# Moving the side stream's transfers and the merges' loads from SyncE's queue to GpSimd's

## The chip, the cores and the metric

The kernel runs on one core of one Trainium2 chip. The metric is the time of one execution on the device in microseconds (us); a kernel is timed in several runs, and one execution more is taken by the hardware profiler. The engines are TensorE (PE), VectorE (DVE), ScalarE (ACT), GpSimd (POOL) and SyncE (SP). Each has its own instruction stream and works in order. A DMA is issued by an instruction in the stream of SP, ACT or POOL, which waits there until what the transfer needs (its data, its free buffer) is there; everything behind it in that stream waits too.

## The reference

One encoder layer and a final norm on two independent sequences (`x_prompt`, `x_sample`) of 1024 tokens by 1024 features, float32:

```python
h = rmsnorm(x, norm1_g)
u_h, q, k, v, g_h, g_a = split(h @ w_in)
filt = hyena_filters(...)             # small MLP with sines, times a decay
y_h = hyena_mixer(u_h, ..., filt)     # short conv, then two rounds of: FFT convolution, times a gate
y_a = window_attention(rope(q), rope(k), v, sink)   # 8 heads, 2 kv heads, blocks of 128
merged = sigmoid(g_h) * (y_h @ w_up_hyena) + sigmoid(g_a) * (y_a @ w_up_attn)
x = x + merged @ w_out
h = rmsnorm(x, norm2_g)
x = x + (silu(h @ w_ff_gate) * (h @ w_ff_up)) @ w_ff_down
return rmsnorm(x, final_g)
```

## The kernel before

Every large product is done in three float32r matmuls (`row`, lines 716 to 718): weight and input are split into a high part (cast on ACT, line 465) and a low rest (subtraction on DVE, line 466).

The program has a main stream and a side stream, both Python generators, which `mix` weaves into one program order with a rate for each stage. The order of each engine's instructions is this program order.

- The main stream is the projections of sample 0, then of sample 1 (`proj_u`, `proj_qkv`, `proj_gates`), the merges (`merge_up`, `merge_out`) for four half sequences, and the two feed-forward blocks. Weights come in tiles of 512 KB through three buffers (`weights`, line 704, on SP).
- The side stream runs beside the projections and the first merges: `filters` (the filter MLP, then the spectra of the filters, stored to memory as `kd`), `hyena(0)`, `attention(0)`, `hyena(1)`, an early part of the merge, and `attention(1)`.

What the change touches:

- Filters: `wo` (line 405) and `dcy` (line 418) share five buffers (`DB = 5`); DVE multiplies the product of `wo` with `dcy` (line 419). `hb` is a bias row. `keep` copies each spectrum group to `ks` (two buffers, lines 427 and 428 on ACT) and stores it to `kd` (line 434).
- `mats` (line 482) loads the 8 matrices of one discrete Fourier transform, `dft_f` or `dft_i`; three times `dft_f`, twice `dft_i`.
- Convolutions: for each of 8 groups, `back` loads the stored spectrum `K` (line 572, two buffers, `KB = 2`), and DVE multiplies with it (line 575). `x2` (line 645) is the second gate, and `yh` (line 649) the stored result; the load of the input `z` and of the first gate `x1` stay on SP.
- Attention: `qb` (line 1071, two buffers) is a block of queries, `ya` (line 1164) the stored result; the loads of all keys and values (`kv`, lines 1065 and 1066) stay on SP.
- Merges: `pair_of` (line 1681) loads two rows of gates (`gin`) or of residuals (`xres`) into the tag `t4`, which has three buffers (`TB = 3`) and also holds squares. ACT applies tanh to the gate tile (line 1187), DVE multiplies it with the product in PSUM (line 1197), adds the two branches (line 1200), and the sum is split again (lines 465 and 466). The rows of `yh` and `ya` come through `y_row` (line 1173, on SP), the finished residual goes out as `xs` (line 1215, on SP). `early_merge` (lines 1049 and 1051) loads the first rows and the first gate ahead.

Issued by POOL already are the loads of the feed-forward input (`sides_in`, line 1297, tile `r`), in the last third of the program. All other DMAs are on SP, but for three on ACT at the start.

The framework that builds the program places the waits: an instruction waits on semaphores that other engines and the DMAs count up. `dynamic_dma_scratch_size=1024` is the room for POOL's transfer descriptors.

Of the kernel before, what the change touches and what calls it, by code (L numbers as in the profile page):

```python
# [21 lines left out]
P = 128  # L22
# [13 lines left out]
CH = 256  # L36
# [14 lines left out]
HALVES = (slice(0, 512), slice(512, 1024))  # L51
# [205 lines left out]
class Kern:  # L257
# [138 lines left out]
    def filter_spectra(self, cpool, hs):  # L396
        nc, a = self.nc, self.a
        mf = self.mats(cpool, "dft_f")
        self.full.clear()
        for o in range(2):  # L400
            ws = []
            for d in range(2):
                wo = cpool.tile([P, DH], F32, tag="dcy", name="wo", bufs=DB)
                for r in range(2):
                    nc.sync.dma_start(wo[64 * r:64 * r + 64], a["filt_w_out"][0].rearrange("k (d o c) -> k d o c", d=2, o=2)[:, d, o])
                ws.append(self.split(cpool, wo, [P, DH], f"ws{d}", bufs=1))
            yield 1.0
            for h in range(2):
                kt = cpool.tile([P, 16, CH], F32, tag="kt", name="kt")
                for r in range(2):  # L410
                    for j in range(0, 8, 2):
                        ps = self.psm()
                        for i in range(2):
                            for k in range(2):
                                nc.tensor.matmul(ps[:, CH * i:CH * i + CH], hs[r][:, P * (j + i):P * (j + i) + P], ws[r][k][:, CH * h:CH * h + CH], start=(i == 0 and k == 0), stop=(k == 1), skip_group_check=i > 0)
                        s = slice(8 * r + j, 8 * r + j + 2)
                        dcy = cpool.tile([P, 2, CH], F32, tag="dcy", name="dcy", bufs=DB)
                        nc.sync.dma_start(dcy, a["decay"][h, :, s])
                        nc.vector.tensor_tensor(kt[:, s], ps.rearrange("p (i c) -> p i c", i=2), dcy, ALU.mult)
                        yield KY  # L420
                hb = cpool.tile([1, CH], F32, tag="hb", name="hb", bufs=1)
                nc.sync.dma_start(hb, a["hyena_bias"][:, o, CH * h:CH * h + CH])
                nc.vector.tensor_tensor(kt[0:1, 0], kt[0:1, 0], hb, ALU.add)

                def keep(g, X, dst=self.kd[o][h]):
                    ks = cpool.tile([P, 4, CH], F32, tag="ks", name="ks", bufs=2)
                    nc.scalar.copy(ks[:, 0:3:2], X)
                    nc.scalar.activation(ks[:, 1], X[:, 1], AF.Copy, scale=-1.0)
                    if g == 0:
                        nc.scalar.copy(ks[:, 3], X[:, 0])  # L430
                        nc.vector.tensor_copy(ks[0:1, 3], X[0:1, 1])
                        nc.vector.memset(ks[0:1, 1:3], 0.0)
                    n = 4 if g == 0 else 3
                    nc.sync.dma_start(dst[:, g, :n], ks[:, :n])
                    yield 0.0

                sx = cpool.tile([P, 8, CH], F32, tag="sx", name="sx")
                for part, op in ((0, ALU.add), (1, ALU.subtract)):
                    nc.vector.tensor_tensor(sx, kt[:, 0:8], kt[:, 8:16], op)
                    yield 2.4  # L440
                    for p in self.spectrum(cpool, sx, part, mf, keep):
                        yield p if isinstance(p, float) else 1.1
# [34 lines left out]
    def mats(self, pool, name):  # L477

        m = {}
        for g in (0, 4, 2, 6, 1, 7, 3, 5):  # L480
            m[g] = pool.tile([P, 4 if g == 0 else 3, P], F32, tag=f"{name}{g}", name=f"{name}{g}", bufs=1)
            self.nc.sync.dma_start(m[g], self.a[name + "0"][0] if g == 0 else self.a[name][g - 1])
        return m

    def spectrum(self, pool, x, part, mf, then):
# [77 lines left out]
    def conv(self, pool, z, o, h, fm, mf, mi, late=None):  # L563
        nc = self.nc
        B = {}

        def tmp(tag, n):
            return pool.tile([P, n, CH], F32, tag=tag, name=tag, bufs=1)

        def back(g, X):  # L570
            K = pool.tile([P, 3, CH], F32, tag="K", name="K", bufs=KB)
            nc.sync.dma_start(K, self.kd[o][h][:, g, 0:3])
            t1 = pool.tile([P, 2, CH], F32, tag="t1", name="t1", bufs=YB)
            t2 = pool.tile([P, 2, CH], F32, tag="t2", name="t2", bufs=1)
            nc.vector.tensor_tensor(t2, X[:, ::-1], K[:, 1:3], ALU.mult)
            yield 0.4
            if g == 0:
                Kd = pool.tile([P, CH], F32, tag="Kd", name="Kd", bufs=1)
                nc.sync.dma_start(Kd, self.kd[o][h][:, 0, 3])
                nc.vector.tensor_tensor(t1[:, 0], X[:, 0], K[:, 0], ALU.mult)  # L580
                nc.vector.tensor_tensor(t1[:, 1], X[:, 1], Kd, ALU.mult)
            else:
                nc.vector.tensor_tensor(t1, X, bc(K[:, 0], 2, 1), ALU.mult)
            yield 0.4
            nc.vector.tensor_tensor(t1, t1, t2, ALU.add)
            ys = self.both(pool, t1, g, "Ys")
            yield LAG_Y
            if not fm:
                r = yield from self.dft("sb", mi[g], t1, ys, g)
                B[g] = pool.tile([P, 2, CH], F32, tag="B", name="B", bufs=4)  # L590
                nc.scalar.copy(B[g], r)
            else:
                r = yield from self.dft_across("sb", mi[g], t1, ys, g)
                B[g] = pool.tile([P, 2, CH], F32, tag="B", name="B", bufs=4)
                nc.scalar.copy(B[g].rearrange("p c (t n) -> p t c n", t=2), r)

        y = pool.tile([P, 8, CH], F32, tag="z", name="y", bufs=2)
        for part in range(2):
            groups = []
            for p in self.spectrum(pool, z, part, mf, back):  # L600
                if isinstance(p, float):
                    yield p
                    continue
                groups.append(p)
                if len(groups) < 4:
                    yield 3.3 if len(groups) > 1 else 1.0
            if part and late:
                late()
            for p in groups[:2]:
                yield p  # L610
            st = inv_even(nc, B, y, tmp) if part == 0 else inv_odd(nc, B, y, tmp)
            for c in st:
                if c is None:
                    break
                yield c
            for p in groups[2:]:
                yield p
            for c in st:
                yield c or 0.5
        return y  # L620
# [5 lines left out]
    def convolutions(self, pool, s):  # L626
        nc = self.nc
# [11 lines left out]
        for h in range(2):  # L639
# [2 lines left out]
            y = yield from self.conv(pool, zs[h], 0, h, False, mf, mi)  # L642
            nc.vector.tensor_tensor(y, y, x1, ALU.mult)
            x2 = pool.tile([P, 2, 8, P], F32, tag="gx", name="gx", bufs=1)
            nc.sync.dma_start(x2, self.x2f[s][2 * h:2 * h + 2].rearrange("t p (n m) -> p t n m", n=8))
            yield 1.5
            yf = yield from self.conv(pool, y, 1, h, True, mf, mi, None if h else lambda: load(1))
            nc.vector.tensor_tensor(x2, x2, yf.rearrange("p n (t m) -> p t n m", t=2), ALU.mult)
            nc.sync.dma_start(self.yh[s][2 * h:2 * h + 2].rearrange("t p (n m) -> p t n m", n=8), x2)
            yield 1.5  # L650


# [389 lines left out]
    def early_merge(self, pool, into, rows):  # L1042

        nc = self.nc
# [1 line left out]
        yy = self.yy.__enter__()  # L1046
        raw = [pool.tile([P, 2, 512], F32, tag=t, name="yraw", bufs=1) for t in ("rf", "ar")]
        for i, t in enumerate(raw):
            nc.sync.dma_start(t, self.yh[0][2 * i:2 * i + 2, :, HALVES[0]].rearrange("j p n -> p j n"))
        g = yy.tile([P, 2, 512], F32, name="gin")  # L1050
        nc.sync.dma_start(g, self.gt[0][0:2, :, HALVES[0]].rearrange("j p n -> p j n"))
        into.append(g)
        yield 0.4
        for t in range(4):
# [7 lines left out]
    def attend(self, pool, s):  # L1062
        nc = self.nc
# [3 lines left out]
        qs = {}  # L1067

        def load(b):
            qs[b] = pool.tile([P, 8, HD], F32, tag="qb", name="qb", bufs=2)  # L1070
            nc.sync.dma_start(qs[b], self.qkv[s][:, b, 0:512].rearrange("p (h e) -> p h e", h=8))

        load(0)
        vv = pool.tile([P, NB, NKV, 2, HD], F32R, name="vv")
# [8 lines left out]
        for b0 in range(0, NB, 4):  # L1083
# [3 lines left out]
            q = slice(P * b0, P * b0 + 512)  # L1087
# [18 lines left out]
    def heads(self, pool, s, b, g, qb, kh, kl, vv):  # L1106

        nc = self.nc
# [52 lines left out]
        for r in range(2):  # L1161
            f = lambda t: t.rearrange("p (a r q) -> p a r q", a=2, r=2)[:, :, r]
            nc.vector.tensor_tensor(oo[64 * r:64 * r + 64], f(po[0:64]), f(ol), ALU.add)
        nc.sync.dma_start(self.ya[s][2 * g:2 * g + 2, :, P * b:P * b + P].rearrange("t p q -> p t q"), oo)


    def y_row(self, yp, tmp, u, i, t):
# [432 lines left out]
    def main(self, outs):  # L1600
# [69 lines left out]
        with tc.tile_pool(name="pb", bufs=TB, reuse_waits="tile") as tmp:  # L1670
# [3 lines left out]
            with tc.tile_pool(name="ya", bufs=1, reuse_waits="tile") as yp, tc.tile_pool(name="ma", bufs=1, reuse_waits="tile") as pool:  # L1674
                def pair_of(c, u, jp):
# [2 lines left out]

                    def load():
                        t = tmp.tile([P, 2, 512], F32, tag="t4", name="xres" if c == "o" else "gin")  # L1680
                        nc.sync.dma_start(t, src[:, :, tok].rearrange("j p n -> p j n"))
                        return t

                    return load
# [144 lines left out]
```

## Time and profile before

| | |
|---|---|
| time, median of 3 runs | 2856.88 us (2856.84 to 2857.31) |
| profiled execution: time | 2856.86 us |
| its span, first to last instruction | 2855.1 us |
| mean granted TensorE clock | 0.997 |
| PE busy | 2822.5 us, 99% |
| DVE busy | 2109.1 us, 74% |
| ACT busy | 1226.2 us, 43% |
| POOL busy | 74.9 us, 3% |
| DMA of SP's queue (q1) | 435.04 MB |
| DMA of POOL's queue (q0) | 73.41 MB |

Busy time is the share of the span in which an engine worked on an instruction; issuing a DMA and waiting are not counted for SP. Matmuls overlap in the pipeline, so a PE that is 99% busy may still start fewer of them than it could, and the number of matmuls started in a stretch says more. A row of waits names the engine and the line that waited, what it waited for, the total, how often, and the longest wait. In a timeline row stand start, duration, engine, line and operation, and in brackets the idle time before it and what ended it. For DMAs, the landing is the time from the issue until the data has arrived.

### The profile page before, as it was taken

The page shows a single profiled execution, that of the slowest core. Times are in us where ns is not written, and L with a number is a line of the kernel's source. Part 1 is how long each engine was busy: PE and PEld are TensorE (multiplying, and loading weights), DVE is VectorE, ACT ScalarE, POOL GpSimd, SP SyncE. Part 2 cuts the span into 40 slices and gives each one's busy share as a digit, 9 for nine tenths or more (in the row PEclk, how much of TensorE's full clock was granted, in tenths as well). Part 3 has the DMA queues.
Part 4 walks back from the last instruction along what each step waited for, and adds up shares of the span by engine and source line. Part 5 has one row for each costly group of instructions (what it writes and reads, how often), then busy time and mean ns, then how long its engine had stood idle before and what let it go on. Part 6 is the DMA issues. An engine that isn't in the chain of part 4 may idle for free.

```text
span 2855.1 us, 36264 instructions
## 1 busy us (share of the span) xinstructions
PE 2822.5 (99%) x13522; PEld 2337.8 (82%) x13522; DVE 2109.1 (74%) x3395; ACT 1226.2 (43%) x1996; POOL 74.9 (3%) x146
## 2 busy tenths in 40 slices
PE   9999999999999999999999999999999999999998
PEld 7789888888898888777787888888888888888887
DVE  7987887877768887978686767775656766676566
ACT  6444222348743334887444444443122444443122
POOL 0000000000000000000000000001112000001100
PEclk9999999999999999999999999999999999999999
DMA  5566564442154435545674436558466434448631
GB/s 164 176 223 243 188 214 156 163 137 82 66 181 128 158 124 186 170 138 176 217 232 163 155 118 223 219 222 307 179 243 258 162 118 152 154 159 323 267 147 67
DMA packets 204029, 510.90 MB, mean 179 GB/s; under 512 B 18663, under 2 KB 70027, under 8 KB 203853
## 3 DMA queue, kind: packets, MB, share of 16 engines
q1 hardware_dynamic: 183261, 435.04, 44.3%
q0 software_dynamic: 20160, 73.41, 6.5%
q8 instruction: 107, 1.75, 0.3%
q14 instruction: 69, 0.57, 0.1%
q10 hardware_dynamic: 432, 0.14, 0.0%
HBM read 350.69 MB, written 157.83 MB: 178 GB/s over the span
## 4 chain that ended last, share of the span: by engine, by line
PE 84%; DVE 6%; DMA 4%; ACT 4%; issue 1%; SPq 0%; DVEq 0%; ACTq 0%
PE mm L716 8%; PE mm L717 8%; PE mm L718 8%; PE mm L1344 4%; PE mm L1346 4%; PE mm L1345 4%; PE sc L529 2%; PE mm L1546 1%; PE mm L1547 1%; PE mm L1545 1%; PE mm L993 1%; PE mm L994 1%; PE sb L1346 1%; PE sb L1345 1%; PE sb L1344 1%; PE mm L992 1%
## 5 line engine op out<-in xcount | busy, mean ns | idle before, releaser
L465 ACT CAST whi<-raw 128x1024 fp32r<-128x1024 f32 (+3 forms) x274 | 265.5, 970 | 524.1 <-PE mm L717 167.2
L466 DVE TENSOR_TENSOR wlo<-raw,whi 128x1024 fp32r<-128x1024 f32 (+3 forms) x274 | 306.4, 1119 | 152.7 <-ACT whi L465 152.1
L716 PE MATMUL mm<-hh,whi 128*128 128x512 f32 x872 | 360.0, 413 | 1.7 <-ACT hh L848 1.6
L718 PE MATMUL mm<-hh,wlo 128*128 128x512 f32 x872 | 349.8, 401 | 0.0
L717 PE MATMUL mm<-hl,whi 128*128 128x512 f32 x872 | 349.5, 401 | 0.0
L465 ACT CAST whi<-s 128x1024 fp32r<-128x1024 f32 x104 | 109.2, 1050 | 251.1 <-PE mm L1345 59.7
L1346 PE MATMUL mm<-r,wlo 128*128 128x512 f32 x518 | 201.6, 389 | 0.0
L1345 PE MATMUL mm<-r,whi 128*128 128x512 f32 x518 | 201.6, 389 | 0.0
L1344 PE MATMUL mm<-r,whi 128*128 128x512 f32 x518 | 201.5, 390 | 0.0
L716 PEld LDWEIGHTS mm<-hh,whi 128*128 128x128 f32 x872 | 164.3, 189 | 33.1 <-ACT hh L848 2.4
L718 PEld LDWEIGHTS mm<-hh,wlo 128*128 128x128 f32 x872 | 164.2, 188 | 33.0 <-issue 0.2
L717 PEld LDWEIGHTS mm<-hl,whi 128*128 128x128 f32 x872 | 164.6, 189 | 29.8 <-issue 0.5
L466 DVE TENSOR_TENSOR wlo<-s,whi 128x1024 fp32r<-128x1024 f32 x104 | 127.0, 1221 | 14.7 <-ACT whi L465 14.1
L1297 POOL DMA_DIRECT2D r<-comb x112 | 59.4, 530 | 2581.2 <-PE mm L1346 1965.2
L1344 PEld LDWEIGHTS mm<-r,whi 128*128 128x128 f32 x518 | 97.2, 188 | 20.7 <-ACT c L1411 0.4
L1345 PEld LDWEIGHTS mm<-r,whi 128*128 128x128 f32 x518 | 97.3, 188 | 20.1
L1346 PEld LDWEIGHTS mm<-r,wlo 128*128 128x128 f32 x518 | 97.2, 188 | 20.1
L994 PE MATMUL mm<-whi,hl 128*128 128x256 f32 x384 | 112.0, 292 | 0.0
L993 PE MATMUL mm<-wlo,hh 128*128 128x256 f32 x384 | 110.5, 288 | 0.0
L992 PE MATMUL mm<-whi,hh 128*128 128x256 f32 x384 | 109.5, 286 | 0.0
L716 PE MATMUL mm<-yh,whi 128*128 128x512 f32 x256 | 101.8, 400 | 4.2 <-DVE gin L1197 2.8
L717 PE MATMUL mm<-yl,whi 128*128 128x512 f32 x256 | 101.6, 397 | 3.5 <-DVE yl L466 3.5
(583 smaller groups left out, 7136.6 us busy)
## 6 DMA issues: line engine op xcount, KB each, us to landing
r<-comb POOLq DMA_DIRECT2D x112, 512.0 KB, 9.4
comb<-stage SPq DMA_DIRECT2D x48, 1024.0 KB, 4.9
K<-kd SPq DMA_DIRECT2D x64, 384.0 KB, 3.2
raw<-in_w_fg SPq DMA_DIRECT2D x44, 512.0 KB, 4.5
raw<-in_w_fu SPq DMA_DIRECT2D x44, 512.0 KB, 3.6
raw<-in_w_g SPq DMA_DIRECT2D x32, 512.0 KB, 3.6
gt<-ge SPq DMA_DIRECT2D x32, 512.0 KB, 3.0
raw<-in_w_up SPq DMA_DIRECT2D x32, 512.0 KB, 4.0
```

What stands on the lines that cost most here:

```text
L465: self.nc.scalar.copy(hi, src)
L466: self.nc.vector.tensor_tensor(lo, src, hi.bitcast(F32), ALU.subtract)
L716: mm(ps, hi[:, k], xh[:, s], start=first, stop=False)
L717: mm(ps, hi[:, k], xl[:, s], start=False, stop=False)
L718: mm(ps, lo[:, k], xh[:, s], start=False, stop=last)
L992: nc.tensor.matmul(ps[:, q], xh[:, t], wh, start=(i == 0), stop=False)
L993: nc.tensor.matmul(ps[:, q], xh[:, t], wl, start=False, stop=False)
L994: nc.tensor.matmul(ps[:, q], xl[:, t], wh, start=False, stop=(i == 7))
L1297: self.nc.gpsimd.dma_start(t.bitcast(F32), src[q][PLACE[name]])
L1344: mm(ps, hi[:, k], xh, start=(first and k == 0), stop=False, skip_group_check=not first)
L1345: mm(ps, hi[:, k], xl, start=False, stop=False, skip_group_check=not first)
L1346: mm(ps, lo[:, k], xh, start=False, stop=(k == n - 1), skip_group_check=not first)
```

## The change

Fourteen calls of `nc.sync.dma_start` become `nc.gpsimd.dma_start`; nothing else differs. With them the listed transfers are issued by POOL's stream, in the same order among themselves. Sizes, buffers and the program order stay.

```diff
@@ filter_spectra
-  nc.sync.dma_start(wo[64 * r:64 * r + 64], a["filt_w_out"][0]...)
+  nc.gpsimd.dma_start(wo[64 * r:64 * r + 64], a["filt_w_out"][0]...)
-  nc.sync.dma_start(dcy, a["decay"][h, :, s])
+  nc.gpsimd.dma_start(dcy, a["decay"][h, :, s])
-  nc.sync.dma_start(hb, a["hyena_bias"][:, o, CH * h:CH * h + CH])
+  nc.gpsimd.dma_start(hb, a["hyena_bias"][:, o, CH * h:CH * h + CH])
-  nc.sync.dma_start(dst[:, g, :n], ks[:, :n])
+  nc.gpsimd.dma_start(dst[:, g, :n], ks[:, :n])
@@ mats
-  self.nc.sync.dma_start(m[g], self.a[name + "0"][0] if g == 0 else self.a[name][g - 1])
+  self.nc.gpsimd.dma_start(m[g], self.a[name + "0"][0] if g == 0 else self.a[name][g - 1])
@@ conv, back
-  nc.sync.dma_start(K, self.kd[o][h][:, g, 0:3])
+  nc.gpsimd.dma_start(K, self.kd[o][h][:, g, 0:3])
-  nc.sync.dma_start(Kd, self.kd[o][h][:, 0, 3])
+  nc.gpsimd.dma_start(Kd, self.kd[o][h][:, 0, 3])
@@ convolutions
-  nc.sync.dma_start(x2, self.x2f[s][2 * h:2 * h + 2]...)
+  nc.gpsimd.dma_start(x2, self.x2f[s][2 * h:2 * h + 2]...)
-  nc.sync.dma_start(self.yh[s][2 * h:2 * h + 2]..., x2)
+  nc.gpsimd.dma_start(self.yh[s][2 * h:2 * h + 2]..., x2)
@@ early_merge
-  nc.sync.dma_start(t, self.yh[0][2 * i:2 * i + 2, :, HALVES[0]]...)
+  nc.gpsimd.dma_start(t, self.yh[0][2 * i:2 * i + 2, :, HALVES[0]]...)
-  nc.sync.dma_start(g, self.gt[0][0:2, :, HALVES[0]]...)
+  nc.gpsimd.dma_start(g, self.gt[0][0:2, :, HALVES[0]]...)
@@ attend
-  nc.sync.dma_start(qs[b], self.qkv[s][:, b, 0:512]...)
+  nc.gpsimd.dma_start(qs[b], self.qkv[s][:, b, 0:512]...)
@@ heads
-  nc.sync.dma_start(self.ya[s][2 * g:2 * g + 2, :, P * b:P * b + P]..., oo)
+  nc.gpsimd.dma_start(self.ya[s][2 * g:2 * g + 2, :, P * b:P * b + P]..., oo)
@@ main, pair_of
-  nc.sync.dma_start(t, src[:, :, tok].rearrange("j p n -> p j n"))
+  nc.gpsimd.dma_start(t, src[:, :, tok].rearrange("j p n -> p j n"))
```

More of the change, by code (lines that the diff above doesn't have):

```diff
@@ L404, in filter_spectra @@
                 for r in range(2):
-                    nc.sync.dma_start(wo[64 * r:64 * r + 64], a["filt_w_out"][0].rearrange("k (d o c) -> k d o c", d=2, o=2)[:, d, o])
+                    nc.gpsimd.dma_start(wo[64 * r:64 * r + 64], a["filt_w_out"][0].rearrange("k (d o c) -> k d o c", d=2, o=2)[:, d, o])
                 ws.append(self.split(cpool, wo, [P, DH], f"ws{d}", bufs=1))
@@ L644, in convolutions @@
             x2 = pool.tile([P, 2, 8, P], F32, tag="gx", name="gx", bufs=1)
-            nc.sync.dma_start(x2, self.x2f[s][2 * h:2 * h + 2].rearrange("t p (n m) -> p t n m", n=8))
+            nc.gpsimd.dma_start(x2, self.x2f[s][2 * h:2 * h + 2].rearrange("t p (n m) -> p t n m", n=8))
             yield 1.5
@@ L648, in convolutions @@
             nc.vector.tensor_tensor(x2, x2, yf.rearrange("p n (t m) -> p t n m", t=2), ALU.mult)
-            nc.sync.dma_start(self.yh[s][2 * h:2 * h + 2].rearrange("t p (n m) -> p t n m", n=8), x2)
+            nc.gpsimd.dma_start(self.yh[s][2 * h:2 * h + 2].rearrange("t p (n m) -> p t n m", n=8), x2)
             yield 1.5
@@ L1048, in early_merge @@
         for i, t in enumerate(raw):
-            nc.sync.dma_start(t, self.yh[0][2 * i:2 * i + 2, :, HALVES[0]].rearrange("j p n -> p j n"))
+            nc.gpsimd.dma_start(t, self.yh[0][2 * i:2 * i + 2, :, HALVES[0]].rearrange("j p n -> p j n"))
         g = yy.tile([P, 2, 512], F32, name="gin")
-        nc.sync.dma_start(g, self.gt[0][0:2, :, HALVES[0]].rearrange("j p n -> p j n"))
+        nc.gpsimd.dma_start(g, self.gt[0][0:2, :, HALVES[0]].rearrange("j p n -> p j n"))
         into.append(g)
@@ L1070, in load @@
             qs[b] = pool.tile([P, 8, HD], F32, tag="qb", name="qb", bufs=2)
-            nc.sync.dma_start(qs[b], self.qkv[s][:, b, 0:512].rearrange("p (h e) -> p h e", h=8))
+            nc.gpsimd.dma_start(qs[b], self.qkv[s][:, b, 0:512].rearrange("p (h e) -> p h e", h=8))
         load(0)
@@ L1163, in heads @@
             nc.vector.tensor_tensor(oo[64 * r:64 * r + 64], f(po[0:64]), f(ol), ALU.add)
-        nc.sync.dma_start(self.ya[s][2 * g:2 * g + 2, :, P * b:P * b + P].rearrange("t p q -> p t q"), oo)
+        nc.gpsimd.dma_start(self.ya[s][2 * g:2 * g + 2, :, P * b:P * b + P].rearrange("t p q -> p t q"), oo)
     def y_row(self, yp, tmp, u, i, t):
```

## The prediction

> **What bounds the kernel now.** I read the page first, then the busy time by stretch, then who makes TensorE (PE) wait, and last the chain.
>
> ```profile
> span 2855.1 us, 36264 instructions
> ...
> PE 2822.5 (99%) x13522; PEld 2337.8 (82%) x13522; DVE 2109.1 (74%) x3395; ACT 1226.2 (43%) x1996; POOL 74.9 (3%) x146
> 1400.00:1500.00 100.00, 95.64 (x423) 77.91 (x421) 85.17 (x120) 53.72 (x72) 0.00 (x0) 1.00 0.70 228
> 2000.00:2100.00 100.00, 98.31 (x434) 81.12 (x433) 57.00 (x67) 16.90 (x17) 19.05 (x36) 1.00 0.63 242
> 2300.00:2400.00 100.00, 100.00 (x443) 82.81 (x442) 69.59 (x90) 43.41 (x58) 0.00 (x0) 1.00 0.42 147
> ```
>
> PE is busy for 2822.5 of 2855.1 us, so it idles 32.6 us in all, start and end included. That is the whole purse: moving transfers can't win more. In an undisturbed stretch PE starts 443 matmuls in 100 us; between 1400 and 1500, in the merges, it starts 423 and idles 4.4 us. The change reaches PE only through waits like these:
>
> ```profile
> PE mm L717 <- DVE yl L466: 3.5, 3, 1.6
> PE mm L716 <- DVE gin L1197: 2.8, 1, 2.8
> ...
> PE mm L716 <- ACT yh L465: 1.4, 1, 1.4
> ...
> PE tr L776 <- DVE ns L753: 0.4, 1, 0.4
> ```
>
> Columns: total, times, longest (us). All four rows are in the merges. ScalarE (ACT) works in order: its tanh on a gate tile (gin, L1187) waits for that tile's load, and the cast of a y row (yh) behind it, or the VectorE (DVE) work that needs the gate, comes late. The next fence shows it: ACT's total wait for gate loads and that for weights of the projections, and the first and the last of five gate loads (4 to 6 us each, at 1186, 1315, 1396, 1417 and 1492 us) among the longest pieces of the chain that ended last (start, length).
>
> ```profile
> ACT gin L1187 <- DMA gin<-gt: 23.0, 11, 4.4
> ...
> ACT whi L465 <- DMA raw<-in_w_u: 0.2, 1, 0.2
> 1186.55 3.80 DMA gin<-gt
> ...
> 1492.84 5.78 DMA gin<-gt
> ```
>
> Weights do not appear this way: 0.2 us is all that ACT or DVE wait for a weight of the projections or merges. So what SyncE's (SP's) queue holds up in front of the weights costs nothing visible today, and taking it away wins nothing there.
>
> **The change part by part.** No work goes. By the table of DMA issues, 294 transfers leave SP's queue for POOL's: 64 K, 8 Kd, 32 kd stores, 32 dcy, 4 hb, 8 wo, 40 dft matrices, 4 x2 loads, 4 yh stores, 3 of the early merge, 31 gin, 16 xres, 16 qb and 32 ya stores. The order among the moved ones stays, so each is behind fewer others than before. POOL's own loads of r start at 1964.6 us, some 400 us after the last moved one, and are not delayed. What a moved transfer pays is a later issue and another landing:
>
> ```profile
> L1681 SPq DMA_DIRECT2D gin<-gt x8: 360/374/462, 1385.8 to 1427.7; - x8
> DMA to landing us min/median/max: 4.4/5.4/5.6
> L1297 POOL DMA_DIRECT2D r<-comb x112: 527/527/670, 1964.6 to 2718.8; - x112
> r<-bs POOLq DMA_DIRECT2D x1, 512.0 KB, 3.5
> r<-comb POOLq DMA_DIRECT2D x1, 512.0 KB, 5.0
> r<-comb POOLq DMA_DIRECT2D x1, 512.0 KB, 7.8
> 2086.54 0.39 PE L1547 MATMUL mm<-r,wlo 128*128 128x512 f32 x1
> 2087.34 0.53 POOL L1297 DMA_DIRECT2D r<-comb  x1 [2.87 <-PE mm L1547]
> 1416.58 0.69 DVE L466 TENSOR_TENSOR ml<-gin,mh 128x512 fp32r<-128x512 f32 x1
> 1417.29 0.38 SPq L1681 DMA_DIRECT2D gin<-gt  x1
> ```
>
> The first two rows are eight gate loads on SP between 1380 and 1440 (issue in ns, landing in us); the third is POOL's issue; then the landing of the first load of a POOL burst, with nothing of its queue before it, at 2141, 2021 and 1964 us. Issue time: 294 x 0.527 = 155 us of POOL in some 1450 us, hidden, as POOL has no other work there; if that cover were gone, it would be those 0.53 us for each. From release to issue SP takes 0.02 us (1416.58 + 0.69 = 1417.27, then 1417.29), POOL 0.41 (2086.54 + 0.39 = 2086.93, then 2087.34). From issue to landing, 512 KB take 4.4 to 5.6 (middle 5.4) on SP in this dense stretch and 3.5 to 7.8 (middle 5.0) on POOL. So the extra latency d of a gate load lies between 0.41 + 3.5 - 5.42 = -1.5 and 0.41 + 7.8 - 4.42 = +3.8 us; the middles give 0.0. The POOL row of 5.0 is from a stretch with 242 GB/s, nearest to the merges' 228. But a gate load has two rows of 2 KB for each partition where r has one of 4 KB, a form that no row of POOL shows; one more 0.53 us of issue for it would make d 0.5. I round up, because POOL's burst of 1964 is long: d = 0.6.
>
> By the Trainium skill, DMA: Bandwidth & Descriptors, section "Latency and other measured facts", the first byte comes some 1 us after a POOL issue and some 0.6 us after an SP one. With POOL's later issue that is an estimated d of 0.8, and the sum below would be 1.0 us higher; the middles here, 5.0 on POOL against 5.4 on SP, don't show that difference under load.
>
> Merges: five waits of PE follow a late gate load and have no slack left, since PE already waits: yl twice (the third yl wait, at 1177, follows ACT's own work), yh, gin and ns. Each grows by d: 5 x 0.6 = 3.0 us. The load at 1186.55 is on the chain without such a wait after it; half counts, 0.3. The xres loads are issued a product pair ahead and nobody waits for one: nothing, or 0.6 each if that cover goes.
>
> ```profile
> 2021.83 2.30 POOL L1297 DMA_DIRECT2D r<-comb  x4 [18.20 <-PE sa L1455]
> 2024.57 1.77 POOL L1297 DMA_DIRECT2D r<-comb  x3 [0.44 <-issue]
> 2027.15 0.53 POOL L1297 DMA_DIRECT2D r<-comb  x1 [0.81 <-DMA r<-comb]
> 247.26 0.33 SPq L434 DMA_DIRECT2D kd<-ks  x1
> 250.35 0.59 ACT L427 COPY ks<-sa 128x512 f32<-128x512 f32 x1
> DMA to landing us min/median/max: 2.4/3.2/4.3
> DVE kt L419 <- DMA dcy<-in_decay: 2.3, 2, 1.7
> PE sd L415 <- DVE kt L419: 0.4, 1, 0.4
> DVE t L575 <- DMA K<-kd: 0.5, 1, 0.5
> 1110.03 1.20 SPq L1051 DMA_DIRECT2D gin<-gt  x1
> 1111.28 0.88 SPq L1065 DMA_DIRECT2D kv<-qkv  x1
> PE sd L1086 <- DMA kv<-qkv: 0.6, 1, 0.6
> ```
>
> In flight: POOL issues seven transfers (4 + 3) and holds the eighth until one has landed. In the merges three tiles (TB = 3) allow three gate or residual loads, so seven is enough; the bursts of 8 and 16 matrices reach it, and their tail is held for about 2 us ahead of wo and dcy, most of it behind earlier work: 0.3 us.
>
> Filters: a kd store's buffer is taken again 250.35 - 247.26 = 3.1 us after its issue at the tightest, and the store lands after 3.2 (the row is of ks). With d it comes 0.6 us late; six such tight pairs of the 16, and half of the delay ends in PE at about one in three: 6 x 0.6 x 0.5 / 3 = 0.6. A dcy load makes DVE wait twice and PE once: once d on PE, 0.6. Bounds: nothing, if DVE makes up for it, and 6 x 0.6 + 2 x 0.6 = 4.8, if all passes through.
>
> Convolutions: DVE has waited 0.5 us for a K load in 64. With d more the tight ones (about 16) wait up to 0.6 each, bounds 0 and 9.6; DVE idles a fourth of the time and PE has main matmuls between, so 0.3. The x2 loads and yh stores have tens of us.
>
> Attention: the kv load no longer waits for the 1.20 us in which SP issued gin ahead of it, which is more than PE's 0.6 us of wait: -0.6. The qb loads and ya stores are used many us later: nothing.
>
> Sum: 3.0 + 0.3 + 0.3 + 0.6 + 0.6 + 0.3 - 0.6 = +4.5 us. The profiled execution took 2856.86 us (span 2855.1), the median of three is 2856.88; 2856.86 + 4.5 = 2861.4 us. The measurement tells about 0.2% (5.7 us) from no change, so this counts as the same: 2851.2 to 2862.6.
>
> **The rivals.** Slower: POOL's landing under the merges' load is like the burst at 1964, not like that of 2021. At d = 2.0 (0.41 + 7.0 - 5.4) the five waits cost 10.0, the other terms, which go with d, grow from 1.8 to 6.0: 2856.9 + 0.3 + 16.0 - 0.6 = 2872.6 us. It decides from d = 0.8, where the sum passes 5.7. For it: the row of 7.8, and a form of two rows that no POOL row shows. Against: two of the three bursts landed within 5.0.
>
> Faster: a gate load's 5.4 us are partly a wait behind the weights, y rows and stores that SP issued just before it; on a queue of its own it lands in the 3.5 us of the row at 2141, d is -1.5, and the waits shrink instead: 5 x 1.5 = 7.5, but no more than they are (yl 3.5 - 1.6, gin 2.8, yh 1.4, ns 0.4 = 6.5), and 0.6 of kv: 2856.9 - 7.1 = 2849.8 us. It needs d below about -1.0. For it: gate loads elsewhere on SP land in under 4 us, as the 3.80 at 1186. Against: the 5.0 at 2021.
>
> By the Trainium skill, DMA: Bandwidth & Descriptors, section "Queues, rings and completion order", a DMA engine takes turns between its queues, packet by packet; by that a gate load on POOL's queue would not stand behind SP's backlog but share with it, as in this rival. The same page says under "Issuing engines are not separate DMA queues" that only issue time is saved. The trace's landings don't decide between them.
>
> No effect: the loads land as on SP (d = 0.0, as the middles say), and only kv and the doubled issue remain: within 1 us of 2856.9.
>
> **How the numbers follow.** Chances: my sum (d about 0.3 to 1.0) 0.43, slower rival 0.29, no effect 0.16, faster rival 0.12. The likeliest gives 2861.4 us, by itself 2858 to 2865. Of it about a third lies above 2862.6. So slower: 0.29 + 0.13 = 0.42, less 0.02 for a weak form of the rival, 0.40; faster: 0.11, as the rival can end short of its limit; same: 0.49. The range that leaves one in ten on each side is 2851 to 2872.
>
> **What would show it.** After: waits of ACT's tanh for gin above 23.0 us by about 11 x 0.6 = 6.6; the four PE rows of the merges above their 3.5, 2.8, 1.4 and 0.4; gin landing 4.8 to 5.4 us after a POOL issue of 0.5 to 1.1 us; PE's wait for kv gone; weights still waited for by nobody; DVE's wait for K under 10 us in all. Gate loads that land in under 4 us would prove the faster rival, over 7 the slower one. The prediction is wrong if PE gains a wait in the convolutions or filters that is not in today's list, or if DVE's or PE's instructions themselves change their duration.

## The result, and the profile after

The changed kernel took 2904.1 us (median of 4 runs, 2901.3 to 2907.57), the kernel before beside it 2856.86 us (4 runs, 2856.41 to 2857.31). The ratio is 1.0163, 95% interval 1.0151 to 1.0176: 47 us slower. The forecast was 2861.4 us with a range up to 2872.

The page of the profiled execution after (2906.14 us):

```profile
span 2903.7 us, 36394 instructions
...
PE 2843.3 (98%) x13522; PEld 2349.3 (81%) x13522; DVE 2111.6 (73%) x3395; ACT 1227.6 (42%) x1996; POOL 250.7 (9%) x440
```

The span grew by 48.6 us. PE's idle time grew from 32.6 to 60.4 us; but PE's busy time grew too, by 20.8 us, with the same 13522 matmuls. So two things are to be explained. First the idle part, by PE's list of waits after (total, times, longest):

```profile
PE sb L525 <- DVE t L585: 10.7, 2, 6.3
PE sd L1086 <- DMA kv<-qkv: 4.4, 1, 4.4
PE mm L716 <- ACT hh L848: 4.2, 1, 4.2
PE sd L525 <- DVE A L144: 4.0, 2, 2.9
PE sc L1156 <- ACT ph L473: 3.9, 7, 1.2
PE mm L716 <- ACT yh L465: 2.8, 2, 2.6
```

Only the last two rows are in the stretch of the merges, on which the prediction spent its working. The others are in the convolutions (the first inverse transform of a hyena stage waits for the product with K), at the start of the second attention (kv), at the start of the program (hh) and in the filters (A). Of these only kv (0.6) and hh (1.6) were in the list of before. Second, the busy part, by the windows of PE: before, then after (start and end, length, PE busy and matmuls, granted clock, share of the DMA engines, GB/s).

```profile
280.00:300.00 20.00, 19.99 (x138) 1.00 0.82 268
300.00:320.00 20.00, 19.98 (x101) 1.00 0.57 181
860.00:880.00 20.00, 19.94 (x89) 1.00 0.47 145
```

```profile
280.00:300.00 20.00, 15.35 (x112) 0.93 0.98 386
300.00:320.00 20.00, 18.25 (x79) 0.64 0.23 72
860.00:880.00 20.00, 15.69 (x77) 0.83 0.54 197
1140.00:1160.00 20.00, 15.58 (x65) 0.85 0.81 288
1460.00:1480.00 20.00, 17.11 (x65) 0.91 0.70 220
```

Around each long stop of PE the granted clock is below 1.00. A stop costs its length, and something after it. Cut finer, the clock is either whole or half. In the kernel before it is half three times: for 3.4 us at 11 us, for 3.4 us at 1503 us, and behind the last matmuls. The changed kernel has the same three (the second at 1472 us) and four longer stretches, of 6.8, 17.1, 6.8 and 6.8 us; this is PE inside them:

```profile
208.70:215.40 6.70, 5.89 (x17) 0.50 0.00 0
301.75:314.40 12.65, 12.65 (x49) 0.50 0.25 73
867.50:874.20 6.70, 4.54 (x13) 0.50 0.49 149
1154.20:1160.90 6.70, 4.67 (x15) 0.50 1.01 379
```

PE works 27.8 us at half clock there. By an estimate from these rows, half of that, 13.9 us, is lost by the clock.

**Where the time is lost.** Every kernel here runs the same matmuls of the main stream (lines 716 to 718, 992 to 994, then the feed-forward lines), so the start of the k-th of them in one trace can be subtracted from its start in the trace of before. The table gives the median of this delay in the stretch of 30 to 300 us that begins at each point (us), for all runs told of below:

| POOL issues | engine order | 50 | 250 | 400 | 800 | 950 | 1050 | 1500 |
|---|---|---|---|---|---|---|---|---|
| all (after) | new | 5.5 | 14.2 | 27.7 | 28.5 | 34.9 | 34.9 | 49.0 |
| all (e1) | old | 7.0 | 12.4 | 11.9 | 14.6 | 15.0 | 15.0 | 28.2 |
| none (e2) | new | 0.5 | 8.0 | 22.0 | 21.8 | 28.5 | 28.5 | 35.9 |
| merges (e3) | own | -1.4 | -0.4 | -0.3 | -0.3 | -0.3 | -0.3 | 7.7 |
| filters, matrices (e4) | own | 5.4 | 10.2 | 11.2 | 11.1 | 12.3 | 12.3 | 12.5 |
| convolutions (e5) | own | -1.1 | -0.6 | 0.4 | 0.3 | -0.4 | -0.4 | 3.3 |
| convolutions (e6) | old | -1.9 | -0.7 | 0.9 | 1.3 | 1.4 | 1.4 | 3.1 |
| attention, early merge (e7) | own | -1.7 | -1.9 | -2.2 | 2.3 | 2.3 | 2.3 | 5.4 |
| all but matrices, early merge (e8) | old | 5.5 | 12.2 | 11.7 | 11.6 | 11.6 | 11.6 | 27.6 |
| all but K, Kd (e9) | own | 7.3 | 12.0 | 14.7 | 17.6 | 16.9 | 16.9 | 34.2 |
| all but matrices (e10) | own | 4.7 | 10.5 | 10.1 | 10.2 | 9.5 | 9.5 | 25.2 |
| merges (e11) | old | -2.0 | -2.1 | -2.8 | -2.8 | -2.7 | -2.7 | 4.0 |
| all but wo, dcy, hb, matrices (e12) | old | -1.2 | 2.3 | 2.2 | 2.4 | 2.8 | 2.8 | 14.5 |

e3 and e11 move nothing ahead of 1120 us and still stand at -0.3 and -2.7 there: a step under 2 us means nothing. Behind 1500 us no delay changes by more than 1.2 us. The changed kernel loses some 6 to 7 us at the start (5.5, where runs without early POOL loads stand between -2.0 and 0.5), 9 in the filters, 13.5 at the start of the first hyena stage (250 to 400), 6.4 at the start of the second (800 to 950), and 14 from the early merge to the end of the merges.

**A correction.** The section on the kernel before said that the order of each engine's instructions is the program order of the generators. It isn't. The framework that places the waits also reorders each engine's stream when it builds the program, and the engine that issues a transfer enters into that; by what rule isn't shown here. In the built program of the changed kernel 1814 of PE's instructions stand at another place than in that of the kernel before, up to 83 places earlier. The moved transfers changed places among themselves too: 28 of the 294. "New" in the table is that order, "old" that of the kernel before, "own" what the build gives the kernel.

### The profile page after: what moved, and what is told of

Same layout as the page of the kernel before. It is cut to its first block, busy times and chain, and to the rows that moved or that the text cites. A ratio compares the mean times of both kernels' runs of the same rounds, so it can differ in the third digit from the quotient of the medians.

```text
span 2903.7 us, 36394 instructions
## 1 busy us (share of the span) xinstructions
PE 2843.3 (98%) x13522; PEld 2349.3 (81%) x13522; DVE 2111.6 (73%) x3395; ACT 1227.6 (42%) x1996; POOL 250.7 (9%) x440
## 4 chain that ended last, share of the span: by engine, by line
PE 73%; DVE 5%; DMA 4%; ACT 4%; issue 3%; POOL 1%; SPq 0%; DVEq 0%; POOLq 0%; ACTq 0%
PE mm L717 7%; PE mm L716 7%; PE mm L718 7%; PE mm L1344 4%; PE mm L1346 4%; PE mm L1345 4%; PE mm L1547 1%; PE mm L1546 1%; PE mm L1545 1%; PE sb L1344 1%; PE sb L1346 1%; PE sb L1345 1%; PE sa L1344 1%; PE sa L1345 1%; PE sa L1346 1%
## 5 line engine op out<-in xcount | busy, mean ns | idle before, releaser
L466 DVE TENSOR_TENSOR wlo<-raw,whi 128x1024 fp32r<-128x1024 f32 (+3 forms) x274 | 306.8, 1120 | 154.6 <-ACT whi L465 153.8
L465 ACT CAST whi<-s 128x1024 fp32r<-128x1024 f32 x104 | 109.2, 1050 | 250.6 <-PE mm L1345 59.7
L466 DVE TENSOR_TENSOR wlo<-s,whi 128x1024 fp32r<-128x1024 f32 x104 | 127.1, 1222 | 14.8 <-ACT whi L465 14.2
```

Source lines behind the costliest of these rows:

```text
L465: self.nc.scalar.copy(hi, src)
L466: self.nc.vector.tensor_tensor(lo, src, hi.bitcast(F32), ALU.subtract)
```

## The experiments

**Order or transfers?** Two theories. O: the new order puts the side stream's instructions too early and PE stops at them. L: POOL's transfers land late, whatever the order. The two are parted by building the program twice: once to read an order, then again with each instruction of PE, DVE and ACT pinned behind its forerunner in it (no wait is added, only the order; lines of a pinned kernel lie up to 4 further down). The edit, shortened:

```diff
+    for name, engine in order:          # of the program built first
+        if engine in ENGINES:           # PE, DVE, ACT
+            if engine in last:          # NoSync: order alone
+                tc.add_manual_dep(traced[name], last[engine], NoSync, reason="order")
+            last[engine] = name
```

e1 has all 294 transfers on POOL and the old order:

> All 294 transfers on POOL, as in the changed kernel, but PE, DVE and ACT issue in the order that the build gave the kernel before. Theory O (the build's planner, told that the transfers are POOL's, puts the side stream's instructions earlier into PE's order, and PE stops at them): the stops at the starts of the filters and of the two hyena stages go (some 30 of the 47 us); what is left is the start of the program (5.5 us, early matrices beside the input loads) and the merges (3 to 6 us): 2863 to 2872 us. Rival L (the transfers themselves land too late, whatever the order): the time stays with the changed kernel, 2895 to 2907 us. In between: both share it.

e2 has all on SP and the new order:

> All transfers on SP, as in the kernel before, but PE, DVE and ACT issue in the order that the build gave the changed kernel. Theory O in its pure form (the order alone costs it): PE stops at the same places, 2880 to 2895 us. Rival L (late landings on POOL): no loss, 2855 to 2860 us. If the early places in the order cost only because POOL's transfers come late, both this run and the one with POOL and the old order are near the kernel before.

e1 took 2885.1 us (ratio 1.010, 1.0085 to 1.0115), e2 2890.0 us (1.012, 1.0105 to 1.0136), where the kernel before took 2856.3. Neither theory alone: late transfers cost 29 us with the old order, the order alone costs 34 us with SP's queue. But the table says where. With the old order both steps at the hyena stages are gone (12.4 to 11.9, 14.6 to 15.0); with the new order both are there, on SP too (8.0 to 22.0, 21.8 to 28.5). The start goes with POOL (7.0 against 0.5). In the filters either costs by itself, POOL 5.4 us and the order 7.5, and both together 8.7. Behind 1050 us POOL alone costs 13.2, the order alone 7.4 and both 14.1 us.

**Which part?** Single parts on POOL, everything else on SP, in the build's own order, and the convolutions with the old order as well:

> Only wo, dcy, hb, the kd stores (lines 405, 418, 422, 434) and the 40 matrices (line 482) on POOL. Theory O and the delays in the changed kernel's trace: start 5.5, filters 11, start of the first hyena stage up to 12, of the second up to 6: 2873 to 2891 us. Rival L alone (my prediction's terms): 2858 to 2864 us.

> Only the convolutions' K, Kd, x2 and yh (lines 572, 579, 645, 649) on POOL, order as the build makes it (859 of PE's instructions stand elsewhere than in the kernel before, the earliest 62 places earlier). Theory O: PE stops at the starts of the two hyena stages, 10 to 20 us: 2866 to 2876 us. Rival L (late landings): K lands in about the same 3 us when little else runs, so under 2859 us, as my prediction had it (0.3 us).

> The same transfers on POOL as in the run with the convolutions alone, but PE, DVE and ACT issue in the order of the kernel before. Theory O: 2855 to 2859 us, so the difference between the two runs is the order. Rival L: the same time as with the build's own order.

> Only the early merge's loads (lines 1049, 1051) and the attention's qb and ya (lines 1071, 1164) on POOL. The theory that the DMA engines take turns between the two queues, so that the kv load on SP now shares with the gate and qb loads instead of standing ahead of them: PE's wait for kv at the start of the second attention grows from 0.6 to 3 or 4 us, and the time to 2860 to 2864 us. My prediction (kv is freed of SP's 1.2 us): 2855 to 2857 us.

e4 took 2869.8 us (1.0047, 1.0030 to 1.0064), e5 2858.8 (1.0011, 1.0001 to 1.0020), e6 2856.6 (1.0004, 0.9995 to 1.0014), e7 2862.7 (1.0022, 1.0013 to 1.0031). With e3 below, the single parts sum to 13.5 + 2 + 6 + 8.5 = 30 us, not 47. e4 lies between its two forecasts. e7 is inside its own (2860 to 2864 us), but by luck: PE's wait for kv, which was to grow to 3 or 4 us, is 1.0, and 4.5 of the 6 us come near 640 us, at the start of the first attention (table: -2.2 to 2.3), where PE waits 2.7 us for uc instead of 0.6; why it does stays open. Theory O fails at the hyena stages: in e5 the first inverse transform stands 62 matmuls of the main stream earlier than before, in e4 91, in the changed kernel 71; yet e4 and e5 lose 1 us at the first hyena stage, the changed kernel 13.5. An early place costs next to nothing by itself there.

**The first K behind the matrices.** What e4 and e5 have in common, and the changed kernel and e2 lack: the 16 matrices and the K loads of a hyena stage are on different queues. POOL's timeline after (start, length, issue; in brackets idle time and what ended it), then DVE's and PE's:

```profile
277.77 0.54 POOL L434 DMA_DIRECT2D kd<-ks  x1 [1.66 <-ACT ks L428]
278.34 2.85 POOL L482 DMA_DIRECT2D dft_f<-in_dft_f  x5
283.70 0.54 POOL L482 DMA_DIRECT2D dft_f<-in_dft_f  x1 [2.51 <-DMA kd<-ks]
...
292.57 0.54 POOL L572 DMA_DIRECT2D K<-kd  x1
```

```profile
299.41 0.69 DVE L575 TENSOR_TENSOR t<-sd,K 128x512 f32<-128x512 f32 x1 [6.56 <-DMA Kd<-kd]
...
301.01 0.68 DVE L585 TENSOR_TENSOR t<-t,t 128x512 f32<-128x512 f32 x1
```

```profile
301.75 0.79 PE L525 MATMUL sb<-t,dft_i 128*128 128x256 f32 x1 [6.35 <-DVE t L585]
```

After the last kd store POOL issues the 16 matrices; their issues take 9.1 us, and 5 us more it stands still, 2.51 of them until a kd store has landed. K goes out 14.8 us behind the store (292.57 - 277.77). DVE has idled 6.56 us when its product with K can start (the profile names Kd, issued just behind K, as the last to land), and PE 6.35 us when the product is there. The kernel before has the same queueing on SP, and pays nothing:

```profile
263.32 0.32 SPq L434 DMA_DIRECT2D kd<-ks  x1
...
279.30 0.60 SPq L572 DMA_DIRECT2D K<-kd  x1
```

There K is 16.0 us behind the store, and PE starts its first inverse transform at 291.98 us, when it has done 71 more matmuls of the main stream than in the changed kernel. So theory Q: neither the place nor the wait costs alone; an early place with K behind the matrices does. e9 and e10 keep the early place (the order stands up to 99 and 100 places earlier than in the kernel before) and part K from the matrices, the one by moving K back to SP, the other the matrices:

> The changed kernel, in the build's own order, but the K and Kd loads (lines 572, 579) back on SP. Theory Q (at the start of a hyena stage the first K stands on POOL behind 16 matrices that are let go one by one, PE reaches the first inverse transform before it, stops 4 to 7 us and then runs at a lower clock): the two steps of 14 and 7 us at 300 and 860 us go, 2880 to 2889 us. Theory O (the earlier place in PE's order alone costs it; that place is no later here): the time stays at 2898 to 2907 us.

> The changed kernel, in the build's own order, but the 40 matrices (line 482) back on SP. Theory Q: K stands behind nothing on POOL, so the two steps go here too, 2880 to 2889 us. Theory O: 2898 to 2907 us. The start of the program keeps its 5 to 7 us, since wo and dcy are then issued there.

e9 took 2888.3 us (1.0112, 1.0096 to 1.0127), e10 2880.3 (1.0086, 1.0071 to 1.0101). The steps of 13.5 and 6.4 us become 2.7 and -0.7 in e9, -0.4 and -0.7 in e10. K's issues in the windows around the first hyena stage (count, ns, first and last start), e10, then e9:

```profile
L572 POOL DMA_DIRECT2D K<-kd x5: 536/536/541, 274.7 to 298.3; - x5
```

```profile
L572 SPq DMA_DIRECT2D K<-kd x4: 320/375/2958, 272.9 to 294.9; - x4
```

K goes out at 274.7 and 272.9 instead of 292.57. Four cells of this table hold: late place with K behind (before, e1), late place with K free (e6), early place with K free (e4, e5, e9, e10) lose at most 2.7 us; early place with K behind (after, e2) loses 13.5 and 14.0.

**The start and the filters.** With nothing to wait for, POOL issues what it has at once:

```profile
1.47 3.88 POOL L482 DMA_DIRECT2D dft_f<-in_dft_f  x7 [0.17 <-issue]
7.09 0.55 POOL L482 DMA_DIRECT2D dft_f<-in_dft_f  x1 [1.74 <-issue]
```

In the kernel before the first dft_f goes out at 91 us, behind SP's weights. Now it runs beside the input tiles x. Their landing on SP (least, middle, most) and PE's wait for hh, before, then after (4.2 in the list above):

```profile
PE mm L716 <- ACT hh L848: 1.6, 1, 1.6
...
DMA to landing us min/median/max: 5.2/5.7/5.9
```

```profile
L836 SPq DMA_DIRECT2D x<-in_xT x16: 327/348/904, 0.7 to 20.7; - x16
...
DMA to landing us min/median/max: 2.9/9.2/11.8
```

> POOL's transfers with the order of the kernel before on PE, DVE and ACT, as in the run that took 2885 us, but the 40 matrices (line 482) and the early merge's three loads (1049, 1051) back on SP. If the matrices, issued on an idle POOL at the very start, hold up the input there (PE waits 5.3 us longer for hh), and the early merge's loads hold up kv (3.7 us): 2885 less 7 and less 4 to 5, 2872 to 2876 us. If those delays come from wo, dcy and qb: no change, 2882 to 2888 us.

> As the run of 2885 us (all on POOL, order of the kernel before), but wo, dcy, hb (lines 405, 418, 422) and the matrices (482) on SP; the kd stores stay on POOL. The theory that whatever POOL issues into the idle queue at the start takes the input's share of the DMA engines, and that in the filters the dcy loads and kd stores hold each other up on POOL: the step of 7 us at the start and that of 4 to 6 us at 200 us both go, 2871 to 2877 us. If the start comes from something else: 2878 to 2886 us.

e8 took 2878.7 us (1.0084, 1.0065 to 1.0103), between its two forecasts; the start is not the matrices' alone, since wo, dcy and hb then take their place at the head of POOL's queue (table: 5.5). e12 took 2870.8 us (1.0050, 1.0035 to 1.0065), and the start is gone (-1.2; x lands in 5.2/5.5/6.0 us). The step in the filters falls from 6.7 in e8 to 3.5. With the old order, its mechanism is in two rows of the DMA table between 190 and 206 us (count, KB each, middle landing in us), before and e8:

```profile
dcy<-in_decay SPq DMA_DIRECT2D x4, 256.0 KB, 5.0
```

```profile
dcy<-in_decay POOLq DMA_DIRECT2D x7, 256.0 KB, 9.2
```

SP issues five dcy loads in a row there as well, within 4.0 us, and behind them a weight. On POOL five of them and two kd stores go out within 6 us beside SP's traffic (that this is why they land later is likely, not shown), they land in 9.2 us, and DVE waits 5.9 us for one of them (in the kernel before 1.7). In the changed kernel this is weaker: the dcy loads of this stretch land in 6.5 us in the middle, and DVE's longest wait for one is 2.9 us. Its filters lose by the new order as well. e2, with every load on SP, loses 7.5 us there, by the wait of PE for A that the changed kernel has too (4.0 us); and at the start of the second attention, where the changed kernel's PE waits 4.4 us for kv, e2 waits 2.8:

```profile
PE sd L529 <- DVE A L147: 4.8, 2, 2.8
...
PE sd L1090 <- DMA kv<-qkv: 2.8, 1, 2.8
```

How the 9 us of the filters split between the order and the landings isn't shown.

**The merges.** Line 1681 alone, in the build's order and in the old one:

> Only the merges' gate and residual loads (line 1681, 47 transfers) on POOL; everything else on SP, order as the build makes it. By the delay of the k-th main matmul in the trace of the changed kernel, the merges cost 4 to 6 us: 2861 to 2863 us. My prediction's own term for them is 3.3 us (2860.2). If POOL's queue helped them on its own: under 2856.

> Only line 1681 on POOL, as in the run of the merges alone (2865 us), but PE, DVE and ACT issue in the order of the kernel before. If the later issue and landing of the gates cost it (about 0.6 us each, behind which the attention's casts stand on ACT): 2861 to 2866 us. If it was the other order: 2855 to 2859 us.

e3 took 2864.8 us (1.0030, 1.0018 to 1.0041), e11 2862.3 (1.0022, 1.0013 to 1.0032): 6 us come from the transfers; the 2.5 us between the two lie within both intervals. The first row is POOL's issue of a gate load in the kernel after (ns); the others are waits in e11, of ACT and of PE:

```profile
L1681 POOL DMA_DIRECT2D gin<-gt x31: 707/718/727, 1152.8 to 1550.4; - x31
```

```profile
ACT gin L1191 <- DMA gin<-gt: 30.6, 14, 3.9
```

```profile
PE mm L720 <- ACT yh L469: 3.9, 3, 1.5
PE sc L1160 <- ACT ph L477: 3.5, 8, 1.2
PE mm L721 <- DVE yl L470: 2.7, 3, 1.6
PE mm L720 <- DVE gin L1201: 1.9, 1, 1.9
```

ACT waits 7.6 us longer for gates than before (23.0). PE feels it at other places than the four rows of the prediction: yl and gin shrink (3.5 to 2.7, 2.8 to 1.9), but the probabilities of the attention (ph, cast by ACT) make PE wait 3.5 us where it waited 0.8, and yh 3.9 instead of 1.4. In one of the waits for ph, 1.0 us at 1194 us, the cast stands behind a tanh that had waited 1.8 us for its gate; the longest, 1.2 us at 1152 us, has no gate just ahead of it, and its cause stays open. In the changed kernel, with its own order, ACT's wait for gates hardly grows, though PE's for ph does (3.9):

```profile
ACT gin L1187 <- DMA gin<-gt: 23.9, 15, 3.8
```

Of its 14 us behind 1050 us some 6.7 go with kv (4.4 us of stop and, as an estimate, half of the 4.67 us at half clock); the rest is the merges', near what e3 and e11 lose.

**What a stop of PE costs.** PE's busy time had grown by 20.8 us. e13 and e14 put eight stops of chosen length into the kernel before, pinned in its own order, where PE is otherwise 100% busy: a matmul waits for a chain of small memsets on POOL, whose first waits for the matmul ahead of it (shortened; lines lie 7 further down).

```diff
+    chains = [[nc.gpsimd.memset(k.gap, 0.0).ins.name for _ in range(n)] for _, n in STOPS]
...
+    tc.add_manual_dep(traced[chain[0]], mine[place - 1], SYNC, reason="stop")
+    tc.add_manual_dep(traced[mine[place]], chain[-1], SYNC, reason="stop")
```

> The kernel before, with eight stops of PE between 1590 and 1940 us, 50 us apart: PE waits there for a chain of 12, 18, 22, 26, 30, 36, 45 and 60 small memsets on POOL (98 to 102 ns each by the rows of the kernel before, so about 1.2, 1.8, 2.2, 2.6, 3.0, 3.6, 4.5 and 6.0 us and some 0.5 us of handing over each), in the order of the kernel before. Theory C (a long stop of PE is followed by a lower granted clock): clock 1.00 behind the first two or three, 0.91 for 20 us or lower behind the longer ones, and a time of 2895 to 2905 us. Rival (a stop costs its own length): clock 1.00 throughout and some 29 us more, 2883 to 2888 us.

> The same eight stops at the same places with the lengths in the reverse order, longest first. Theory C: the same time within 4 us, and the low clock behind the first places instead of the last. If the clock depends on the place and not on the length, it falls behind the same places as before.

The memsets took longer than planned, so the stops were 2.0 to 9.9 us, 41 us in all, and both runs lie above the forecast of 2895 to 2905 us. e13 took 2913.7 us (1.0201, 1.0163 to 1.0240), e14 2915.0 (1.0206, 1.0176 to 1.0235): 58 and 59 us more, where the stops alone would make 41. PE's busy time in e13 is 2842.0 us, 19.5 more than before. Four of the stops of e13 in the windows of PE, and the first and the last of the eight in its timeline:

```profile
1575.00:1600.00 25.00, 22.99 (x110) 1.00 0.23 83
1630.00:1655.00 25.00, 21.95 (x90) 0.93 0.41 153
...
1740.00:1765.00 25.00, 20.65 (x79) 0.86 0.56 208
...
1975.00:2000.00 25.00, 15.12 (x58) 0.80 0.19 64
```

```profile
1586.14 0.50 PE L1353 MATMUL mm<-r,wlo 128*128 128x512 f32 x1 [2.01 <-POOL gap L1836]
...
1993.07 0.80 PE L1353 MATMUL mm<-r,wlo 128*128 128x512 f32 x1 [9.88 <-POOL gap L1836]
```

By the delay of the main stream's matmuls across each stop, less the stop itself, what comes on top is:

| stop, us | 2.0 | 3.0 | 3.7 | 4.3 | 5.0 | 5.9 | 7.4 | 9.9 |
|---|---|---|---|---|---|---|---|---|
| on top, e13 | 0.1 | 1.8 | 1.7 | 2.7 | 2.8 | 2.5 | 3.0 | 2.4 |
| on top, e14 (reverse order) | 1.8 | 1.8 | 1.7 | 2.9 | 2.4 | 1.9 | 1.8 | 1.7 |

From 3 us on, each stop costs 1.7 to 3.0 us on top, whatever its length and place; at 2 us it does in one run of two. By the Trainium skill, TensorE: Matmul & The Clock Gate, section "HAM oscillation", PE falls to half clock over idle gaps of more than about 3.4 us, and the loss is half of the time at that clock. The trace agrees in kind (the granted clock is 0.50 in the stretches above, and a matmul lasts 0.80 us behind the longest stop, 0.50 behind the shortest), but already 3.0 us suffice here. The changed kernel has six stops of 2.6 to 6.4 us. Behind two of them, at 14 and at 1471 us, the clock is half for 3.4 us, as it is at two places of the kernel before. The other four, of 2.9, 6.4, 4.3 and 4.4 us, go with the four stretches at half clock shown with the result, which by the estimate there cost 2.9, 6.3, 2.3 and 2.3 us, 13.9 of the 20.8. Three of these are what the table of stops says. The stretch at the first hyena stage is 17.1 us long, where the inserted stops have 3.4 to 10.2; why it is longer stays open, and so do the other 7 us.

## Why the prediction was wrong

**"The order among the moved ones stays"** and program order as the order of the engines: this step failed, and with it the 0.3 us for the convolutions, which rested on PE having main matmuls to do while a K is late. Moving a transfer to another engine made the build reorder PE, DVE and ACT, and 71 of these matmuls no longer stood ahead of the first inverse transform. Where the new place met K behind the matrices, PE stopped 6.3 and 4.4 us, some 20 us with what follows a stop (13.5 + 6.4). DVE's waits for K and Kd are 11.0 us in all (said: under 10). With the order held fixed the step itself was right: e6 costs 1 us, its interval holds both nothing and 0.3.

**No term for loads that go out earlier.** The prediction priced every moved transfer as later. At the start the matrices go out 90 us earlier, or wo and dcy in their place (e8), beside the input: 6 to 7 us. It had named the rule for this, that a DMA engine takes turns between its queues (the Trainium skill, DMA: Bandwidth & Descriptors, "Queues, rings and completion order"), but only as a gain for gate loads; the landing of x, 9.2 us instead of 5.7, shows the other side of it.

**Filters, 0.6 + 0.6 us:** mis-sized, and the order left out. The term took d = 0.6 us. The step there is 9 us after, 5 to 7 with POOL's transfers and the old order (e1, e8), beyond the stated upper end of 4.8; in e8 the dcy loads land 4 us later in the dense stretch (9.2 against 5.0), not 0.6. With the new order alone it is 7.5 (e2).

**kv, -0.6 us:** wrong sign. PE's wait for kv grew from 0.6 to 4.4 us. The new order alone makes it 2.8 (e2). Besides, kv now runs beside the gate and qb loads of POOL, which land in 9.9 us there, where SP used to issue them in turn. Which of them matters isn't settled: with POOL the wait is 3.7 in e1, 1.7 with the early merge's loads back on SP (e8), but 2.0 in e12 and 1.0 in e7, which leave them on POOL.

**Merges, 3.3 us:** cause right with the order held fixed, path wrong, size about half. In e11 ACT waits 7.6 us longer for gates (said: 6.6; in the changed kernel 0.9), POOL's issue is 0.72 us (said: 0.53, or twice that), and the whole costs 6.2 us (3.7 to 9.1 by the interval). But PE's waits for yl and gin, which were to grow by d each, shrank. What was missed is that ACT also casts the probabilities of the attention, in one of the waits right behind a late tanh. The slower rival, at 2872.6 us, priced the same five rows higher; it isn't what happened either, since gate loads after land in 4.7 us in the middle (before 4.2).

**No term for the clock:** PE's duration was taken as fixed; 20.8 of the 49 us are PE's own time, by the estimate above 13.9 of them at half clock behind four stops. The prediction named that as a sign of being wrong, and the waits in the convolutions too; both came.

What held, nearly: PE waits 0.5 us for a weight (ACT 3.3 for those of proj_u, where it waited 0.2), ya is waited for by nobody that shows and qb once (by ACT, 4.3 us), and POOL's issue time (175.8 us more of POOL busy) is hidden, but for the 9.1 us of matrix issues ahead of the first K.

## What to carry to other kernels

Moving a transfer to another engine's queue can also change the order that the build gives to every engine: compare the built orders before pricing queues, and pin the old order to tell the two apart. A transfer that leaves a full queue can also go out too early and take bandwidth from what is needed first, and a load that the next step needs must not stand behind a burst on its queue. Price a stop of PE of 3 us or more at its length and some 2 us on top, and look at the granted clock behind it: at one place here it was 6 us on top.

## What the runs showed of the hardware

A POOL issue takes 0.54 us for a load of one row for each partition, 0.72 us for the gate loads of two rows of 2 KB; on SP they take 0.32 and 0.37 us in the middle. And an inserted stop of PE costs 1.7 to 3.0 us beyond its own length from 3 us on, about the same for 3 and for 10 us: the granted clock is 0.50 around it for 3.4 to 10.2 us, part of which PE still idles. At the changed kernel's stop of 6.35 us it is 0.50 for 17.1 us.
